# Three groups of weight sums made by DRAM-to-DRAM transfers, and three blocks of products recomposed

## The chip, the cores and the metric

The kernel runs on one core of a Trainium2 chip. A core has a matrix engine (TensorE, PE in the profile), a vector engine (VectorE, DVE), a scalar engine (ScalarE, ACT), a general engine (GpSimd, POOL) and SyncE (SP), which here only issues transfers. Each engine works through its own queue in order; semaphores make one wait for another. Sixteen DMA engines carry the transfers that SP, ACT and POOL issue. The metric is the device time of one execution in microseconds (us).

## The reference

One transformer block over 256 tokens of width 2048, in fp32. Three kinds of attention are mixed by gates, and a convolved, gated feed-forward layer follows:

```python
h = rms_norm(x, g_mix)
fq, fk, fv, f_logit, sq, sk, sv, mq, gates = split(h @ w_in)
o_fox = forgetting_attention(rms(fq), rms(fk), fv, cumsum(log_sigmoid(f_logit + b)))   # 6 heads of 128
o_sb = stick_breaking_attention(sq, sk, sv)                                            # 6 heads
mk, mv = split(rms_norm(mem, g_mem) @ w_mem_kv)
o_mem = memory_attention(rms(mq), rms(mk), mv)                                         # 4 heads
g = sigmoid(gates.reshape(..., 3, 2048) + b_gate)
x = x + (g[0] * (o_fox @ w_br_fox) + g[1] * (o_sb @ w_br_sb) + g[2] * (o_mem @ w_br_mem)) @ w_out
u = causal_depthwise_conv(rms_norm(x, g_ffn) @ w_up, conv_w, conv_b)                   # 2 x 5632 channels
x = x + (silu(u_gate) * u_val) @ w_down
```

Nearly all of the work is in the products with `w_in`, `w_out`, `w_up` and `w_down`.

## The kernel before

Each fp32 product is made of three matmuls in a faster format: both operands are split into a high and a low half, and `three` multiplies high by high, low by high and high by low (lines 360 to 362). A weight piece arrives by a DMA from SP ("raw"), ACT casts its high half ("hi", line 354, in the up stage line 143), DVE subtracts to get the low half ("lo", line 355 or 144), and PE then uses both. There are four buffers for hi and four for lo, and four to six for raw, so a piece can be some 5 us ahead of PE.

The stages follow one another: keys and values of the memory; the projections of the attentions; the gates (three blocks of 2048 columns, in two halves m = 0 and 1); the branches; the out stage; the up stage, in pieces of two k-tiles by 512 columns, eight for each group of four channel tiles; the down stage in two blocks of 1024 columns, "d0" and "d1".

In the gates, the out stage and the down stage, `blocked` works on pairs of k-tiles (128 rows each), two halves of the tokens and two halves of the columns. A pair is done in one of two ways. An **eight** (`eight`, "e" in a plan) multiplies the 2x2x2 blocks one by one: 8 products, 24 matmuls of 128x512, and splits two weight parts of 128x1024. A **seven** ("s") is a scheme of seven products with sums of activation blocks and sums of weight blocks: 21 matmuls. Its partial results gather in four more PSUM banks `Y`, and after the last seven of a block DVE spreads them (`gathered`, lines 1083 to 1095 for the gates; `gather` in the others).

- In the out and down stages, `seven` reads the weight sums T1 to T4 from DRAM tiles `kept_...`. They were made stages before, by SP loads into SBUF, three DVE adds and an SP store (`half_sums`, `pair_sums_ahead`, `first_sums`). A seven has parts of 1024, 1024, 1024 and 512 columns; the last, T4 (line 453), goes to a scratch tile.
- In the gates, `seven_here` uses sums that `prepared` makes on DVE one step ahead (lines 472 to 475, four adds of 128x512).
- The sums of activations come from `pair_sums` (five or more small DVE operations and ACT casts): for the gates ahead, in the background (`xs`, GS groups), in the down stage at the letter "f" of a plan. In d1 an "f" writes into places of the activations `aT` that d1's eights have used.

The scratch tiles have the name "junk" and rotate over two buffers:

```python
def junk(name):
    return sm.tile([P, 512], F32, tag="junk", bufs=2, name=name)
```

A tile that takes a buffer waits until the last user of that buffer is through. In the down stage, the T4 parts of all sevens are junk tiles.

What sets the order: a scheduler puts instructions on each engine's queue, and those passed to `in_order` keep the order of the program. `tick` runs one step of the generators in `background` and of the queued work (`later`). The up stage has 176 such ticks of 2.77 us.

## Time and profile before

| | us |
|---|---|
| median of 3 runs | 1461.15 (1460.55 to 1462.65) |
| profiled execution | 1460.56 |
| its span in the trace | 1458.8 |
| granted clock of TensorE | 1.000 |
| busy: PE / DVE / ACT / POOL | 1452.1 / 1221.8 / 851.9 / 21.4 |
| DMA | 387.64 MB, 266 GB/s on average |

Where the stages lie, from the trace: memory keys 0 to about 58; gate block 01 (half 0, branch 1) 361 to 402.7 and 02 to 444; up stage 742 to 1232; d0 to about 1344; d1 to 1453; then the last sums and the store.

The profile comes from one execution. In a row of the timeline stand the start, the duration, the engine, the line, the operation, output and inputs, and in brackets how long the engine was idle before and what ended that. A row of the windows gives for each engine the busy time in that stretch, then TensorE's granted clock, the share of the DMA engines' time, and GB/s. A row of PE's waits gives the sum, the number and the longest. The durations of matmuls overlap, and so do those of neighbouring DVE rows a little: the spacing of starts is what counts. A row of the DMA issues ends with the median time from issue to landing.

### The profile page before, as it was taken

Reading aid. Unit: us, or ns where it says so; the run is one execution under the profiler, and the core shown is the slowest. Engines: PE = TensorE matmul, PEld = TensorE weight load, DVE = VectorE, ACT = ScalarE, POOL = GpSimd, SP = SyncE. Lnnn points to the kernel's source line nnn. Section 1 sums busy time; section 2 is a strip of 40 time slices with the busy share of each in tenths; the row PEclk is TensorE's granted clock in tenths of the full one; section 3 lists DMA queues with packets and bytes.
Section 4 is the critical chain, followed back from the end, with each engine's and each line's share of the span. In section 5 each row is a group of like instructions: output and inputs, shape, how many; then the busy total and the mean of one; then the engine's idle time right before and its main releaser. Section 6 shows DMA issues by size and latency. Waiting matters only on the chain.

```text
span 1458.8 us, 20569 instructions
## 1 busy us (share of the span) xinstructions
PE 1452.1 (100%) x7295; PEld 1228.4 (84%) x7295; DVE 1221.8 (84%) x1804; ACT 851.9 (58%) x1210; POOL 21.4 (1%) x52
## 2 busy tenths in 40 slices
PE   9999999999999999999999999999999999999998
PEld 7888878888888888888888888888888888888887
DVE  5788778776898899998987888888888877999878
ACT  6755445464564555546766656556556565676665
POOL 0000010010000000000000000000000000000000
PEclk9999999999999999999999999999999999999999
DMA  8797899777668576788877888888888866789896
GB/s 290 228 352 247 320 323 333 266 250 217 212 206 268 176 226 201 271 266 261 304 213 231 290 275 299 282 270 299 286 278 298 272 197 201 253 283 341 293 334 220
DMA packets 166502, 387.64 MB, mean 266 GB/s; under 512 B 12554, under 2 KB 29854, under 8 KB 162174
## 3 DMA queue, kind: packets, MB, share of 16 engines
q1 hardware_dynamic: 164702, 383.29, 79.2%
q10 hardware_dynamic: 1328, 2.11, 0.4%
q8 instruction: 57, 0.93, 0.3%
q0 software_dynamic: 368, 0.93, 0.2%
q14 instruction: 47, 0.39, 0.1%
HBM read 347.47 MB, written 38.80 MB: 265 GB/s over the span
## 4 chain that ended last, share of the span: by engine, by line
PE 95%; issue 1%; DVE 1%; DMA 1%; SPq 0%; ACT 0%; POOL 0%; DVEq 0%; POOLq 0%; ACTq 0%
PE u L1289 22%; PE u L1290 11%; PE xg L362 4%; PE xg L361 4%; PE xg L360 4%; PE xd L360 4%; PE xd L362 3%; PE xd L361 3%; PE s L362 2%; PE f L360 2%; PE s L360 2%; PE f L362 2%; PE f L361 2%; PE b L362 2%; PE s L361 2%; PE b L361 2%
## 5 line engine op out<-in xcount | busy, mean ns | idle before, releaser
L1289 PE MATMUL u<-hT,hi_u 128*128 128x512 f32 x1232 | 428.5, 394 | 0.0
L1290 PE MATMUL u<-hT,lo_u 128*128 128x256 f32 x1232 | 341.5, 277 | 0.0
L1289 PEld LDWEIGHTS u<-hT,hi_u 128*128 128x128 f32 x1232 | 231.0, 188 | 53.4
L144 DVE TENSOR_TENSOR lo_u<-raw_u,hi_u 128x1024 fp32r<-128x1024 f32 x176 | 215.5, 1225 | 72.1 <-ACT hi_u L143 71.8
L143 ACT CAST hi_u<-raw_u 128x1024 fp32r<-128x1024 f32 x176 | 184.7, 1050 | 132.7 <-PE u L1289 107.0
L1290 PEld LDWEIGHTS u<-hT,lo_u 128*128 128x128 f32 x1232 | 231.5, 188 | 0.0
L355 DVE TENSOR_TENSOR lo_d<-raw_d,hi_d 128x1024 fp32r<-128x1024 f32 x88 | 106.8, 1223 | 16.7 <-ACT hi_d L354 14.3
L354 ACT CAST hi_d<-raw_d 128x1024 fp32r<-128x1024 f32 x88 | 91.8, 1053 | 39.9 <-PE xd L361 14.3
L354 ACT CAST hi_g<-raw_g 128x1024 fp32r<-128x1024 f32 (+1 forms) x80 | 77.0, 972 | 48.5 <-PE xg L361 19.2
L355 DVE TENSOR_TENSOR lo_g<-raw_g,hi_g 128x1024 fp32r<-128x1024 f32 (+1 forms) x80 | 88.7, 1121 | 4.1 <-ACT hi_g L354 4.1
L362 PE MATMUL xg<-lo_g,xT 128*128 128x512 f32 x175 | 68.1, 389 | 0.0
L360 PE MATMUL xg<-hi_g,xT 128*128 128x512 f32 x175 | 68.1, 389 | 0.0
L361 PE MATMUL xg<-hi_g,xT 128*128 128x512 f32 x175 | 68.1, 389 | 0.0
L143 ACT CAST hi_f<-raw_f 128x1024 fp32r<-128x1024 f32 (+1 forms) x40 | 38.5, 966 | 46.3 <-PE f L361 30.7
L144 DVE TENSOR_TENSOR lo_s<-raw_s,hi_s 128x1024 fp32r<-128x1024 f32 (+1 forms) x40 | 44.5, 1119 | 24.4 <-ACT hi_s L143 24.4
L1289 PE MATMUL u<-hT_rest,hi_u 128*128 128x512 f32 x176 | 62.0, 394 | 0.0
L143 ACT CAST hi_s<-raw_s 128x1024 fp32r<-128x1024 f32 (+1 forms) x40 | 38.4, 962 | 38.2 <-PE s L361 26.5
L143 ACT CAST hi_b<-raw_b 128x1024 fp32r<-128x1024 f32 x32 | 33.7, 1052 | 45.4 <-PE b L361 18.6
L1240 ACT ACTIVATE y<-u,taps 128x256 f32<-128x256 f32 x88 | 49.5, 595 | 17.0 <-DVE u L1235 16.8
L144 DVE TENSOR_TENSOR lo_f<-raw_f,hi_f 128x1024 fp32r<-128x1024 f32 (+1 forms) x40 | 44.4, 1117 | 16.9 <-ACT hi_f L143 16.9
L360 PE MATMUL xd<-hi_d,aT 128*128 128x512 f32 x148 | 57.6, 389 | 0.0
L362 PE MATMUL xd<-lo_d,aT 128*128 128x512 f32 x148 | 57.6, 389 | 0.0
(551 smaller groups left out, 3484.0 us busy)
## 6 DMA issues: line engine op xcount, KB each, us to landing
raw_u<-in_w_up_dram SPq DMA_DIRECT2D x176, 512.0 KB, 4.8
raw_g<-in_w_in_dram SPq DMA_DIRECT2D x96, 512.0 KB, 4.5
raw_d<-in_w_down_dram SPq DMA_DIRECT2D x63, 512.0 KB, 5.6
pre_d<-in_w_down_dram SPq DMA_DIRECT2D x17, 1024.0 KB, 7.2
kept_d<-pre_d SPq DMA_DIRECT2D x17, 1024.0 KB, 6.7
raw_f<-in_w_in_dram SPq DMA_DIRECT2D x32, 512.0 KB, 5.8
raw_s<-in_w_in_dram SPq DMA_DIRECT2D x32, 512.0 KB, 6.1
raw_t_d<-kept_d SPq DMA_DIRECT2D x25, 512.0 KB, 5.8
```

Source lines behind the costliest of these rows:

```text
L143: pin(nc.scalar.copy(hi[:, :m], raw[:, :m]))
L144: pin(nc.vector.tensor_tensor(lo[:, :m], raw[:, :m], hi[:, :m].bitcast(F32), ALU.subtract))
L354: nc.scalar.copy(hi[:, :n], src)
L355: nc.vector.tensor_tensor(lo[:, :n], src, hi[:, :n].bitcast(F32), ALU.subtract)
L360: fix(nc.tensor.matmul(o, lhsT=ah, rhs=w[0], start=first, stop=False))
L361: fix(nc.tensor.matmul(o, lhsT=al, rhs=w[0], start=False, stop=False))
L362: fix(nc.tensor.matmul(o, lhsT=ah, rhs=w[1], start=False, stop=last))
L1240: nc.scalar.activation(y, u[:, 2:], AF.Identity, scale=tap(2), bias=tap(3))
L1289: nc.tensor.matmul(ps[i], lhsT=hi[:, j, c], rhs=hT(k + j), start=first, stop=False)
L1290: nc.tensor.matmul(ps[i][:, :S], lhsT=lo[:, j, c], rhs=hT(k + j)[:, :S], start=False, stop=last)
```

## The change

Three groups of weight sums are made by POOL's transfers instead of not at all, and the plans use them. The plans give three pairs more to sevens: one in gate block 01 (the new letter "t": `seven` with kept sums, inside a gate block) and two in d1, whose order of letters changes too, with five "f" where three were. `GS` goes from 3 to 4, so that a fourth group of activation sums is made ahead for each half of the gates.

`sums_in_hbm` copies one column of its last argument into a junk tile on POOL (a mark, which makes what follows wait for that argument), then copies a pair's weights (1 MB) from DRAM into the kept tile, and forms the sums by four accumulating transfers of 256 KB within DRAM. It is called once in the memory keys' stage, and twice by `last_sums` late in the up stage, at ticks 148 and 160.

```diff
-GS = 3
+GS = 4
...
-    g_plans = (("", "esesesee", "esesesee"), ("esesesee", "esesesee", "esesesee"))
+    g_plans = (("", "esesest" + "e", "esesesee"), ("esesesee", "esesesee", "esesesee"))
     d_plans = (
         "efefefef" + "sef" * 4 + "ssefsfssfssee",
-        "efefef" + "sss" + "esss" * 3 + "ssee",
+        "efsss" * 3 + "efssfsssssee",
     )
+    in_hbm = (("d", 1, 14), ("d", 1, 15))
...
         for pr in pairs(name, plan.count("s"))
+        if (name, nb, pr) not in in_hbm
...
+    def sums_in_hbm(name, nb, pr, w, c0, behind):
+        mark = junk(f"mark_{name}_{pr}")[:, :1]
+        in_order(nc.gpsimd.tensor_copy(mark, behind))
+        kept = kept_for(name, nb, pr)
+        b = by_k(w)[:, 2 * pr : 2 * pr + 2, c0 : c0 + PIECE].rearrange("p k (n c) -> p k n c", n=2)
+        in_order(nc.gpsimd.dma_start(kept.rearrange("p (k n) c -> p k n c", k=2), b))
+        for dst, src in ((0, b[:, 0, 1]), (1, b[:, 1, 1]), (3, kept[:, 0]), (2, kept[:, 3])):
+            in_order(nc.gpsimd.dma_start(kept[:, dst], src, accum_op=ALU.add))
+
+    def last_sums(delay, period):
+        for _ in range(delay):
+            yield
+        for name, nb, pr in in_hbm:
+            sums_in_hbm(name, nb, pr, w_down, nb * PIECE, a_done[-1][:, :1].bitcast(F32))
+            for _ in range(period):
+                yield
...
-                by_seven(sp[s], s == 0, s == ns - 1)
+                (seven if c == "t" else by_seven)(sp[s], s == 0, s == ns - 1)
...
             row_rstd(rstd_m, ssm, "m")
+            sums_in_hbm("g", "01", 3, w_in, C_GATE + D, rstd_m[:, :1])
...
+    a_done = []
+    background.append(last_sums(148, 12))
...
-            split_to(a_pair(f // 2)[:, f % 2], g)
+            a_done.append(a_pair(f // 2)[:, f % 2])
+            split_to(a_done[-1], g)
...
-        return a_blocks[:, 2 * (p - N0 + N1) + f // 2, :, f % 2]
+        i = 3 * (p - N0) + f
+        return a_blocks[:, 2 * N1 + i // 2, :, i % 2]
```

The accumulations wait for one another where the second reads what the first wrote: the first waits for the 1 MB copy, the third for the first, the fourth for the third.

How this moves instructions, at three places. In the orders below, a row is a line of the code, an operation, output and inputs with their numbers, and the shape; lines of the changed kernel from 355 on are 19 higher in `parts` and 20 higher in the gates.

**DVE, end of gate block 01.** `lo_g01` are low halves of eights (k-tiles 12 to 15) or of parts of the seven of k-tiles 6 and 7 with `lo_t`, `lo_t4`; `yg01` the partial results that are gathered into `gw` and `g`; `g02` belongs to the next block. Before:

```order
L355 TENSOR_TENSOR lo_g01_12_3713<-raw_g01_12_3710,hi_g01_12_3712 128x1024
L1083 SCALAR_TENSOR_TENSOR g_0_1_0_3729<-yg01_0_3501,scales_111,bg_0_1_3497 128x512
L355 TENSOR_TENSOR lo_g01_13_3737<-raw_g01_13_3734,hi_g01_13_3736 128x1024
L1088 TENSOR_TENSOR gw_0_1_3728<-gw_0_1_3728,yg01_1_3502 128x512
L355 TENSOR_TENSOR lo_g01_14_3759<-raw_g01_14_3756,hi_g01_14_3758 128x1024
L1090 TENSOR_TENSOR gw_0_1_3728<-gw_0_1_3728,yg01_2_3503 128x512
L355 TENSOR_TENSOR lo_g01_15_3779<-raw_g01_15_3776,hi_g01_15_3778 128x1024
```

And in the changed kernel:

```order
L374 TENSOR_TENSOR lo_g01_6_3736<-raw_g01_6_3726,hi_g01_6_3735 128x1024
L374 TENSOR_TENSOR lo_g01_7_3746<-raw_g01_7_3729,hi_g01_7_3745 128x1024
L374 TENSOR_TENSOR lo_t_g01_3_3756<-raw_t_g01_3_3731,hi_t_g01_3_3755 128x1024
L374 TENSOR_TENSOR lo_t4_g01_3_3766<-raw_t4_g01_3_3733,hi_t4_g01_3_3765 128x512
L1103 SCALAR_TENSOR_TENSOR g_0_1_0_3791<-yg01_0_3517,scales_111,bg_0_1_3513 128x512
L374 TENSOR_TENSOR lo_g01_14_3775<-raw_g01_14_3772,hi_g01_14_3774 128x1024
L374 TENSOR_TENSOR lo_g01_15_3799<-raw_g01_15_3796,hi_g01_15_3798 128x1024
L1108 TENSOR_TENSOR gw_0_1_3790<-gw_0_1_3790,yg01_1_3518 128x512
L374 TENSOR_TENSOR lo_g02_6_3833<-raw_g02_6_3830,hi_g02_6_3832 128x1024
```

Where two low halves stood there are four, and the gathering starts behind them, with one eight of its block left instead of two.

**SP, the up stage.** `raw_u36_1_14` is the last weight piece of channel tiles 36 to 39, `raw_u40_0_0` the first of 40 to 43; `raw_t4_d0` are the T4 parts of the first two sevens of d0 (junk tiles). Before, those two stood near the start of the stage:

```order
L142 DMA raw_u0_1_2_7032<-in_w_up_dram 128x2x512
L142 DMA raw_u0_1_4_7060<-in_w_up_dram 128x2x512
L453 DMA raw_t4_d0_0_11976<-kept_d0_0_2252 128x512
L453 DMA raw_t4_d0_1_12067<-kept_d0_1_2414 128x512
L142 DMA raw_u0_1_6_7082<-in_w_up_dram 128x2x512
```

In the changed kernel they stand late in it:

```order
L142 DMA raw_u36_1_12_11281<-in_w_up_dram 128x2x512
L142 DMA raw_u36_1_14_11303<-in_w_up_dram 128x2x512
L472 DMA raw_t4_d0_0_12018<-kept_d0_0_2260 128x512
L472 DMA raw_t4_d0_1_12109<-kept_d0_1_2422 128x512
L142 DMA raw_u40_0_0_11337<-in_w_up_dram 128x2x512
L142 DMA raw_u40_0_2_11381<-in_w_up_dram 128x2x512
```

The two loads moved from the pieces of channel tile 0 to those of tile 40, since the marks take the two junk buffers first.

**POOL, the same place.** Before, nothing follows the two transfers at the start of the up stage. In the changed kernel (an "x2" stands for two transfers in a row):

```order
L1181 DMA rbc_5984<-rstd_row_6931 128x256
L326 COPY mark_d_14_11028<-aT_6779 128x1
L329 DMA kept_d1_14_11030<-in_w_down_dram 256x1x1024
L331 DMA kept_d1_14_11030<-in_w_down_dram 128x512 x2
L331 DMA kept_d1_14_11030<-kept_d1_14_11030 128x512 x2
L326 COPY mark_d_15_11325<-aT_6779 128x1
L329 DMA kept_d1_15_11327<-in_w_down_dram 256x1x1024
```

The second mark stands behind all five transfers of the first group.

More of the change, by code (lines that the diff above doesn't have):

```diff
@@ L403, in blocked @@
         Y = []
-        ns = plan.count("s")
+        ns = plan.count("s") + plan.count("t")
         def a_of(p, j, t):
@@ L451, in seven @@
             nc.sync.dma_start(raw2.rearrange("p (n c) -> p n c", n=2), kept[:, 0:4:3])
-            raw3 = t4_tile(f"raw_t4_{name}{nb}_{p}")
+            raw3 = t4_tile(f"raw_t4_{name}{nb}_{p}")[:, :512]
             nc.sync.dma_start(raw3, kept[:, T4])
@@ L496, in blocked @@
         s, e = 0, 0
-        sp = pairs(name, ns)
+        sp = range(ns) if name == "g" else pairs(name, ns)
         ep = [p for p in range(len(plan) - plan.count("f")) if p not in sp]
         for i, c in enumerate(plan):
-            if c == "s":
+            if c in "st":
                 if s == 0:
```

## The prediction

> **What bounds the kernel now.** I read the page's table of engines first, then PE's waits, then the timeline of PE, and only then the three places that the change touches. The engines' row of the page, and the whole list of what PE waited for:

> ```profile
> PE 1452.1 (100%) x7295; PEld 1228.4 (84%) x7295; DVE 1221.8 (84%) x1804; ACT 851.9 (58%) x1210; POOL 21.4 (1%) x52
> PE spare L93 <- DVE qscale L565: 1.2, 1, 1.2
> PE s L362 <- DVE lo_s L144: 0.8, 1, 0.8
> PE kv L155 <- DVE memT L186: 0.4, 1, 0.4
> PE kv L154 <- ACT memT L183: 0.3, 1, 0.3
> ```

> PE is busy for 1452.1 of 1458.8 us and waits 2.7 us in all, 1.9 of them at the start. So the time is the number of matmuls times their spacing: a removed matmul pays whatever the stage, and any new wait of PE is paid in full. The spacing is read where PE runs without a gap:

> ```profile
> 439.73 0.39 PE L361 MATMUL xg<-hi_g,xT_rest 128*128 128x512 f32 x1
> ...
> 444.26 0.39 PE L360 MATMUL b<-hi_b,oT 128*128 128x512 f32 x1
> ```

> Twenty matmuls start between 439.73 and 444.26: 0.2265 us each, although one is shown as 0.39 long, since they overlap.

> **Term 1, the removed matmuls: -2.04 us.** An eight has 24 products of 128x512, a seven 21. Three eights become sevens (one in the gates' block 01, two in the second down block), so nine matmuls go: 9 x 0.2265 = 2.04 us, 0.14% of the time. Nothing else in the change takes work from PE, so this is the whole gain. A measurement of this kernel tells about 0.2% (2.9 us) from no change; a gain by itself lies under that. The question is what PE has to wait for in exchange.

> **Term 2, the end of gate block 01: DVE.** The new seven has four parts to split where the eight had two, and DVE makes the low half of each. The next block's first seven follows soon behind it. DVE there, and PE's first two uses of that seven:

> ```profile
> 389.29 1.22 DVE L355 TENSOR_TENSOR lo_g<-raw_g,hi_g 128x1024 fp32r<-128x1024 f32 x1
> ...
> 398.75 0.69 DVE L472 TENSOR_TENSOR t_g<-raw_g 128x512 f32<-128x512 f32 x1 [0.58 <-DMA raw_g<-in_w_in_dram]
> ...
> 406.25 0.69 DVE L355 TENSOR_TENSOR lo_g<-raw_g,hi_g 128x512 fp32r<-128x512 f32 x1
> 406.86 0.69 DVE L475 TENSOR_TENSOR t_g<-t_g,raw_g 128x512 f32<-128x512 f32 x1
> 407.46 1.23 DVE L355 TENSOR_TENSOR lo_g<-raw_g,hi_g 128x1024 fp32r<-128x1024 f32 x1
> 408.59 2.36 DVE L355 TENSOR_TENSOR lo_t_g<-t_g,hi_t_g 128x1024 fp32r<-128x1024 f32 x2
> 408.58 0.39 PE L362 MATMUL yg<-lo_g,xT 128*128 128x512 f32 x1
> 409.26 0.39 PE L362 MATMUL xg<-lo_g,xT 128*128 128x512 f32 x1
> ```

> From 389.29 on, where the replaced eight's first split starts, DVE pauses once (0.58, for a DMA) before it is through with the second part at 407.46 + 1.23 = 408.69. PE wants that part at 409.26, so 0.57 us are spare. A split of 1024 occupies DVE for 1.13 (407.46 to 408.59), one of 512 for 0.61 (406.25 to 406.86). The new seven splits three of 1024 and one of 512, 3 x 1.13 + 0.61 = 4.00 us, against 2 x 1.13 = 2.26 for the eight: 1.74 more. The other DVE rows between those two points (the gathering of the block's sums, its scaling, the next block's weight sums) are the same ones in another order. PE for its part comes 3 x 0.2265 = 0.68 earlier. So DVE is late by 1.74 + 0.68 = 2.42, less the pause of 0.58 and the spare 0.57 if both are used up: 1.27 us. That is the lower bound. The upper one keeps the pause, and lets it grow by a little since the transfers stand in the same queue: 2.42 - 0.57 + 0.8 = 2.65. I take +2.0. The fourth set of activation sums that this block needs is made early, beside the gate projection:

> ```profile
> 345.00:365.00 20.00, 20.00 (x90) 16.55 (x89) 11.76 (x16) 8.98 (x10) 0.00 (x0) 1.00 0.58 172
> L369 DVE TENSOR_TENSOR xa<-xT x3: 686/691/692, 164.0 to 311.4; 128x512 f32<-128x512 f32 x3
> ```

> With this add of 0.69 us and four more operations that are no larger it costs DVE at most 5 x 0.69 = 3.5 us, where DVE is idle for 8 of 20: nothing on the path. The cover is that idle time; without it PE would wait up to those 3.5.

> **Term 3, the end of the up stage: SP's queue behind POOL.** Each of the two groups of weight sums begins with a POOL copy into a scratch tile of one column (the mark), which takes the next of two rotating scratch buffers. The first two sevens of the down stage load their last part into the same two buffers, so these two SP loads must now wait for the two marks. In the order of SP they stand between the last piece of channels 36 to 39 and the first of 40 to 43, and what is queued behind them is the whole weight stream of the stage. Before, they were issued at 754.78, long ahead, and the stream ran freely:

> ```profile
> 754.78 0.95 SPq L453 DMA_DIRECT2D raw_t_d<-kept_d  x2
> 1168.07 0.37 SPq L142 DMA_DIRECT2D raw_u<-in_w_up_dram  x1
> 1172.12 0.37 SPq L142 DMA_DIRECT2D raw_u<-in_w_up_dram  x1
> 1157.31 0.41 ACT L177 CAST aT<-y 128x256 fp32r<-128x256 f32 x1 [1.63 <-DVE y L1248]
> 1179.59 1.05 ACT L143 CAST hi_u<-raw_u 128x1024 fp32r<-128x1024 f32 x1 [1.72 <-PE u L1289]
> 1180.68 1.22 DVE L144 TENSOR_TENSOR lo_u<-raw_u,hi_u 128x1024 fp32r<-128x1024 f32 x1 [1.55 <-ACT hi_u L143]
> 1188.02 0.27 PE L1290 MATMUL u<-hT,lo_u 128*128 128x256 f32 x1
> ```

> The first mark waits for the cast that ends at 1157.72, so POOL starts at about 1158.0. The second mark stands on POOL's queue behind the first group's transfers: a copy of 1 MB from DRAM to DRAM, whose landing the first accumulating transfer (256 KB) waits for, whose landing the third waits for, whose landing the fourth waits for before it is issued. The second mark is then free after copy + 2 accumulations + about 1.0 us of issuing and the mark itself. No such transfer is in this trace. The nearest rows, first POOL's own, then SP's (KB each, us to landing):

> ```profile
> ck<-ck_row POOLq DMA_DIRECT2D x1, 512.0 KB, 9.4
> ck<-ck_row POOLq DMA_DIRECT2D x1, 256.0 KB, 7.6
> rbc<-rstd_row POOLq DMA_DIRECT2D x1, 128.0 KB, 6.4
> pre_d<-in_w_down_dram SPq DMA_DIRECT2D x17, 1024.0 KB, 7.2
> raw_d<-kept_d SPq DMA_DIRECT2D x25, 256.0 KB, 5.2
> raw_u<-in_w_up_dram SPq DMA_DIRECT2D x176, 512.0 KB, 4.8
> ```

> Cheapest, by SP's rows: 7.2 + 2 x 5.2 + 1.0 = 18.6, so the second mark comes at 1176.6. Dearest, POOL's line carried on (1.8 more for each 256 KB, so 13.0 for 1 MB) and 8 for an accumulation: 30.0, at 1188.0. I take POOL's rows at their nearest sizes, 9.4 + 2 x 7.6 + 1.0 = 25.6, at 1183.6. SP then issues the held load (0.5) and the first piece of channel 40, which lands 4.8 later; cast and split follow in 2.31 (1179.59 to 1181.90). PE wants it at 1188.02. So the stall is mark + 7.6 - 1188.0: nothing up to a mark at 1180.4, 3.2 us at 1183.6, 7.6 at 1188.0. I take +3.2. The 5 to 7 us that the piece had in hand are the cover here.

> [...]

> **Term 4, the second down block: +0.2 us.** Its last run of sevens grows from five to seven. What the run strains is the transfers:

> ```profile
> 1415.00:1440.00 25.00, 25.00 (x112) 20.69 (x111) 19.66 (x18) 17.20 (x20) 0.00 (x0) 1.00 1.00 349
> ACT hi_d L354 <- DMA raw_d<-in_w_down_dram: 0.6, 2, 0.4
> ```

> The DMA engines are busy throughout. A seven brings 1.835 MB in 21 x 0.2265 = 4.76 us, 385 GB/s, and gets 349. In the fifth seven ACT's cast already waits up to 0.4 us for a load. Two more sevens move that by 0.3 to 0.5 each, against some 1.5 us between a split and its use, of which the fifth seven's third part kept 0.9. Between 0 and 0.5; I take 0.2. The two more forms (activation sums, at most 3.5 us of DVE each, as above) and their copies on ACT, which wait for PE to be through with an eight, stand early in the block, where the next parts are cast ahead; nothing.

> **Term 5, the group made in the memory keys' stage: 0.** It adds a copy and four accumulations on POOL's queue at about 37 us, and on that queue nothing is wanted until 183. Its bytes share the engines with the stage's loads:

> ```profile
> 37.00:47.00 10.00, 10.00 (x53) 8.27 (x52) 7.44 (x10) 5.45 (x11) 0.00 (x0) 1.00 0.80 256
> 1150.00:1175.00 25.00, 25.00 (x147) 21.88 (x146) 22.89 (x38) 15.79 (x26) 0.00 (x0) 1.00 0.80 259
> ```

> A share of 0.80 leaves a fifth free, in both places. If the free fifth were not enough, loads there would come later by a few us at most, and I allow 0.3.

> **Sum.** -2.04 + 2.0 + 3.2 + 0.2 = +3.4 us. The profiled execution took 1460.56 (1458.8 and 1.8 around the span), so 1463.9 for one like it; the median of the three runs stands 0.6 above it, so 1464.5 as a median.

> **Rivals.**
> - Only the gates stall. POOL's transfers are as fast as SP's, the mark comes by 1180.4, SP's held loads are issued in time. Then -2.04 + 2.0 + 0.2 = +0.2: 1461.3. For it: SP's 1 MB in 7.2. Against it: every transfer of POOL in the trace takes longer than one of SP of its size. [...]
> - The covers all hold, and the change gives what it removes: 1461.15 - 2.0 = 1459.1. This is the other side. It turns on DVE at 389 to 409: it must win back 2.42 us, which it can only if PE's stall at the end of the new seven is absorbed by a wait that is shorter than I read, or the loads come earlier and the splits start before 389.29, together with a mark before 1180.4. Nothing in the rows speaks for the first.
> - The chain of transfers is long, at the dear end: -2.04 + 2.65 + 7.6 + 0.5 = +8.7, 1469.9. For it: an accumulation has to read what it adds to, which no row here prices.
> - The sums do not pay since the run of sevens becomes bound by transfers: two more sevens at 349 GB/s take 5.26 instead of 4.76 us each. With seven in a row that is 3.5 us behind, less 1.5 in hand: up to +2 in place of the 0.2. Against it: before's five in a row should then have cost 1 us, and PE has no wait there.

> **How the numbers follow.** Both stalls, gates and SP's queue: 0.55. Gates alone: 0.25. All covers hold: 0.14. Something else (the run of sevens, the memory keys' stage, another order of late things): 0.06. Of the first case, the part with a mark before 1183.1 stays under +2.9 us: 0.15 of the 0.55. Of the last, 0.04 are slower and 0.02 faster. So slower by over 0.2%: 0.40 + 0.04 = 0.44; faster: 0.02 and 0.01 taken from the covers that hold, 0.03, since it needs more than the removed matmuls; within 0.2%: 0.15 + 0.25 + 0.13 = 0.53. The range takes in all covers holding at the low end and the dear chain at the high end: 1459.0 to 1470.0. The most likely case by itself runs from 1461.5 to 1470.

> **What would show it.** PE's list of waits should gain two rows: a matmul of the gates' block 02 that waits for DVE's lo_g for 1 to 2.7 us at about 407 to 409, and one on L1290's successor that waits for lo_u by some 3 us at about 1188. SP's timeline should show a hole between the pieces around 1168, ended by a POOL copy. POOL's DMA rows should show 9 and 7 us. Wrong would be: no hole in SP, the accumulations in 3 us, no wait of PE at 408, or waits of PE behind 1415 for lo_d or lo_t_d.

## The result

The changed kernel takes 1469.76 us in the median of six runs (1467.88 to 1472.12), the kernel before 1460.96 us beside it (1460.13 to 1462.65): a ratio of 1.0061, 95% interval 1.0048 to 1.0074. It is 8.8 us slower. The forecast was 1464.5, slower by 3.4, in a range up to 1470: the direction and the place were right, the size was too small by more than half. By its chances the prediction even held no clear change for likelier (0.53) than a clear loss (0.44). That the time still lies inside the range, 0.2 us below its end, is luck: the end was set by a chain of transfers longer than the one that came.

The profiled execution of the changed kernel is the fastest of the six, 1467.88 us with a span of 1466.2, so its trace explains 7.4 of the 8.8 us; what the slower five had besides is not known. In three of the versions below one execution of eleven stands 7 to 9 us above the median at full clock.

### The profile page after: what moved, and what is told of

Read it like the earlier page. It is cut to its first block, busy times and chain, and to the rows that moved or that the text cites. A ratio compares the mean times of both kernels' runs of the same rounds, so it can differ in the third digit from the quotient of the medians.

```text
span 1466.2 us, 20656 instructions
## 1 busy us (share of the span) xinstructions
PE 1453.6 (99%) x7286; PEld 1230.5 (84%) x7286; DVE 1232.1 (84%) x1831; ACT 859.0 (59%) x1225; POOL 34.5 (2%) x70
## 4 chain that ended last, share of the span: by engine, by line
PE 91%; DMA 4%; DVE 2%; ACT 1%; issue 1%; SPq 0%; POOL 0%; ACTq 0%; DVEq 0%; POOLq 0%
PE u L1312 20%; PE u L1313 10%; PE xg L381 4%; PE xg L380 4%; PE xg L379 4%; PE xd L380 3%; PE xd L379 3%; PE xd L381 3%; PE f L379 2%; PE f L381 2%; PE f L380 2%; PE s L381 2%; PE s L379 2%; PE s L380 2%; PE b L380 2%; PE b L381 2%
## 5 line engine op out<-in xcount | busy, mean ns | idle before, releaser
L1313 PE MATMUL u<-hT,lo_u 128*128 128x256 f32 x1232 | 345.8, 281 | 0.5 <-DVE lo_u L144 0.5
L144 DVE TENSOR_TENSOR lo_u<-raw_u,hi_u 128x1024 fp32r<-128x1024 f32 x176 | 214.9, 1222 | 79.9 <-ACT hi_u L143 79.8
L143 ACT CAST hi_u<-raw_u 128x1024 fp32r<-128x1024 f32 x176 | 184.6, 1050 | 138.5 <-PE u L1312 89.0
L143 ACT CAST hi_f<-raw_f 128x1024 fp32r<-128x1024 f32 (+1 forms) x40 | 38.5, 967 | 47.7 <-PE f L380 26.2
L380 PE MATMUL xg<-hi_g,xT 128*128 128x512 f32 x168 | 65.4, 389 | 0.0
L379 PE MATMUL xg<-hi_g,xT 128*128 128x512 f32 x168 | 65.4, 389 | 0.0
L144 DVE TENSOR_TENSOR lo_s<-raw_s,hi_s 128x1024 fp32r<-128x1024 f32 (+1 forms) x40 | 44.4, 1120 | 23.1 <-ACT hi_s L143 23.1
L143 ACT CAST hi_s<-raw_s 128x1024 fp32r<-128x1024 f32 (+1 forms) x40 | 38.3, 962 | 42.6 <-PE s L380 26.7
L143 ACT CAST hi_b<-raw_b 128x1024 fp32r<-128x1024 f32 x32 | 33.7, 1052 | 44.2 <-PE b L380 20.2
L144 DVE TENSOR_TENSOR lo_f<-raw_f,hi_f 128x1024 fp32r<-128x1024 f32 (+1 forms) x40 | 44.4, 1117 | 17.7 <-ACT hi_f L143 14.9
L373 ACT CAST hi_t_d<-raw_t_d 128x1024 fp32r<-128x1024 f32 (+1 forms) x54 | 43.5, 836 | 19.3 <-PE xd L380 12.1
L373 ACT CAST hi_t_g<-t_g 128x1024 fp32r<-128x1024 f32 x30 | 31.6, 1052 | 38.8 <-PE xg L380 30.9
## 6 DMA issues: line engine op xcount, KB each, us to landing
raw_u<-in_w_up_dram SPq DMA_DIRECT2D x176, 512.0 KB, 4.9
raw_g<-in_w_in_dram SPq DMA_DIRECT2D x95, 512.0 KB, 4.4
raw_d<-in_w_down_dram SPq DMA_DIRECT2D x61, 512.0 KB, 5.9
pre_d<-in_w_down_dram SPq DMA_DIRECT2D x17, 1024.0 KB, 7.5
kept_d<-pre_d SPq DMA_DIRECT2D x17, 1024.0 KB, 6.0
raw_f<-in_w_in_dram SPq DMA_DIRECT2D x32, 512.0 KB, 5.7
raw_s<-in_w_in_dram SPq DMA_DIRECT2D x32, 512.0 KB, 6.0
raw_t_d<-kept_d SPq DMA_DIRECT2D x27, 512.0 KB, 6.1
```

What stands on the lines that cost most here:

```text
L143: pin(nc.scalar.copy(hi[:, :m], raw[:, :m]))
L144: pin(nc.vector.tensor_tensor(lo[:, :m], raw[:, :m], hi[:, :m].bitcast(F32), ALU.subtract))
L373: nc.scalar.copy(hi[:, :n], src)
L379: fix(nc.tensor.matmul(o, lhsT=ah, rhs=w[0], start=first, stop=False))
L380: fix(nc.tensor.matmul(o, lhsT=al, rhs=w[0], start=False, stop=False))
L1313: nc.tensor.matmul(ps[i][:, :S], lhsT=lo[:, j, c], rhs=hT(k + j)[:, :S], start=False, stop=last)
```

## The profile after

The first row is that of the engines, the rest the whole list of what PE waited for in the changed kernel:

```profile
PE 1453.6 (99%) x7286; PEld 1230.5 (84%) x7286; DVE 1232.1 (84%) x1831; ACT 859.0 (59%) x1225; POOL 34.5 (2%) x70
PE u L1312 <- ACT hi_u L143: 4.2, 1, 4.2
PE spare L93 <- DVE qscale L584: 1.2, 1, 1.2
PE xg L381 <- DVE lo_g L374: 0.8, 1, 0.8
PE g L379 <- DVE sb L1009: 0.6, 1, 0.6
PE mq L381 <- DVE lo_mq L144: 0.5, 1, 0.5
PE yg L381 <- DVE lo_g L374: 0.5, 1, 0.5
PE u L1313 <- DVE lo_u L144: 0.5, 1, 0.5
PE kv L776 <- DVE memT L769: 0.3, 1, 0.3
PE kv L155 <- DVE memT L186: 0.2, 1, 0.2
```

There are nine matmuls fewer (7295 before), and new waits: 4.2 and 0.5 us in the up stage, 0.8 and 0.5 at the gates' block 02, 0.6 in the gates' first projection (g) and 0.5 in the memory queries (mq). The 0.8 us for lo_s are absent in this execution.

The end of the up stage, on POOL's queue and then on SP's:

```profile
1159.42 0.61 POOL L326 COPY mark_d<-aT 128x1 f32<-128x1 f32 x1 [387.00 <-ACT aT L177]
1159.97 0.68 POOL L329 DMA_DIRECT2D kept_d<-in_w_down_dram  x1
1168.57 1.76 POOL L331 DMA_DIRECT2D kept_d<-in_w_down_dram  x2 [7.92 <-DMA kept_d<-in_w_down_dram]
1176.81 0.81 POOL L331 DMA_DIRECT2D kept_d<-kept_d  x1 [6.48 <-DMA kept_d<-in_w_down_dram]
1182.53 0.81 POOL L331 DMA_DIRECT2D kept_d<-kept_d  x1 [4.91 <-DMA kept_d<-kept_d]
1183.06 0.48 POOL L326 COPY mark_d<-aT 128x1 f32<-128x1 f32 x1
1170.06 13.84 SPq L472 DMA_DIRECT2D raw_t_d<-kept_d  x2
1184.00 1.88 SPq L142 DMA_DIRECT2D raw_u<-in_w_up_dram  x3
```

POOL waits for three landings on the way, and comes to the second mark at 1183.06. SP sits with the two loads of the down stage from 1170.06 on, and the next weight piece is issued at 1184.00. What that does to ACT and PE, and to TensorE's clock (in the windows: PE's busy time, then PEld, DVE, ACT, POOL, the granted clock, the DMA share, GB/s):

```profile
1192.59 1.04 ACT L143 CAST hi_u<-raw_u 128x1024 fp32r<-128x1024 f32 x1 [11.65 <-DMA raw_u<-in_w_up_dram]
1193.69 0.79 PE L1312 MATMUL u<-hT,hi_u 128*128 128x512 f32 x1 [4.16 <-ACT hi_u L143]
1186.00:1189.00 3.00, 3.00 (x19) 2.63 (x18) 0.00 (x0) 0.00 (x0) 0.00 (x0) 1.00 0.86 264
1189.00:1194.00 5.00, 0.84 (x5) 0.50 (x3) 0.33 (x1) 1.04 (x1) 1.67 (x2) 0.81 1.03 380
1194.00:1196.00 2.00, 1.53 (x5) 0.95 (x5) 1.41 (x2) 1.31 (x2) 0.00 (x0) 0.50 1.07 384
1196.00:1198.00 2.00, 2.00 (x8) 1.71 (x8) 1.90 (x3) 1.32 (x3) 0.00 (x0) 0.50 1.17 212
1198.00:1200.00 2.00, 2.00 (x10) 1.69 (x10) 1.81 (x6) 1.52 (x3) 0.66 (x1) 0.76 1.01 319
```

PE waits 4.16 us. Its clock is at half from 1192.12 to 1198.95 (the edges come from narrower windows), so PE works at half clock for the last 5.3 us of that. PE is shown as busy there, but does 8 matmuls in 2 us where it did 19 in 3 us.

To add up what the waits cost with the refill of the pipeline and the slow clock, I summed, over stretches of 50 us, by how much the starts of matmuls lie farther apart than is usual for their shape. Against the kernel before, the up stage's end costs 7.2 us, the gates' block 02 1.8, the wait at 338 0.9, the one at 67 0.9; the wait for lo_s (1.0) is not there, and the start is 0.5 shorter. With the 2.0 us of the removed matmuls: -2.0 + 7.2 + 1.8 + 0.9 + 0.9 - 1.0 - 0.5 = 7.3, against 7.4 measured. Each of these sums is good to some 0.2 us.

## The experiments

Theory A: the loss is the second mark. It takes a scratch buffer that a load of the down stage wants, that load stands in SP's queue ahead of the weight stream, and the mark stands on POOL's queue behind the first group's landings. Theory B: POOL's 4 MB take bandwidth from the weight stream. A third suspicion is that the gates' part carries the loss.

**Marks first.** Both marks ahead of the transfers; the scratch buffers are shared as before, and the transfers stay:

```diff
         for name, nb, pr in in_hbm:
-            sums_in_hbm(name, nb, pr, w_down, nb * PIECE, a_done[-1][:, :1].bitcast(F32))
+            mark_for(name, pr, a_done[-1][:, :1].bitcast(F32))
+        for name, nb, pr in in_hbm:
+            sums_in_hbm(name, nb, pr, w_down, nb * PIECE, None)
```

> The changed kernel, but both marks are made on POOL before the first group's transfers. The marks stay in the two scratch buffers that the first sevens' loads want, the transfers and their bytes stay. Theory A (SP's weight stream is held by a load that waits for the second mark, and the mark waits on POOL's queue for the first group's landings): the second mark comes at about 1160, SP has no hole, PE's waits of 4.2 and 0.5 us at 1189 to 1195 and the half clock after them (together 7.2 us in the trace of the changed kernel) are gone: about 1461, within 1 us of before. Theory B (the 4 MB that POOL moves there take bandwidth from the weight stream): the same transfers at the same time, so PE still waits about 4 us: 1467 to 1471.

Measured: 1461.21 us, ratio to before 1.0007 (0.9994 to 1.0020; before 1460.31 beside it). POOL, SP and PE's waits in this kernel:

```profile
1158.24 0.94 POOL L326 COPY mark_d<-aT 128x1 f32<-128x1 f32 x2 [386.80 <-ACT aT L177]
1183.74 1.02 POOL L333 DMA_DIRECT2D kept_d<-in_w_down_dram  x1
1158.88 0.81 SPq L478 DMA_DIRECT2D raw_t_d<-kept_d  x2
PE xg L387 <- DVE lo_g L380: 0.8, 1, 0.8
PE mq L387 <- DVE lo_mq L144: 0.5, 1, 0.5
PE yg L387 <- DVE lo_g L380: 0.5, 1, 0.5
PE mq L385 <- ACT hi_mq L143: 0.3, 1, 0.3
```

The two loads wait until 1158.9 and are gone; the second group's copy starts at 1183.74, as late as in the changed kernel, and PE does not wait in the up stage. Theory A holds and B falls: the same transfers at the same time cost PE nothing.

**A tile of its own for the marks.**

```diff
-        mark = junk(f"mark_{name}_{pr}")[:, :1]
+        mark = sm.tile([P, 1], F32, tag="mark", bufs=2, name=f"mark_{name}_{pr}")
```

> The changed kernel with the marks in a tile of their own, so that the two loads of the first sevens stand early in SP's order again, as before the change; POOL's queue is that of the changed kernel, with the second mark behind the first group. Theory A: no hole in SP's stream and no wait of PE at the end of the up stage, about 1461, as with the marks first. Theory B: as slow as the changed kernel, 1467 to 1471.

Measured: 1471.46 us, 1.0079 (1.0065 to 1.0093). Neither theory had this right: there is no wait of PE in the up stage (A), and the time is as long as B said. PE's longest new wait is 0.8 us, and it has a clock of 1.0. Instead, its matmuls are farther apart, 0.233 us in the down stage instead of 0.227. I put the new tile at 64 bytes of each partition, by which all tiles behind it in memory, the activations of the branches, the out stage and the down stage among them, begin later. No trace shows an address or that size (two buffers of one column alone hold 8 bytes): the shift is read from the tile and from the order in which the kernel opens its pools. That it costs time was a guess at this point; two runs test it.

**The marks in a tile that is there and unused** (160 columns that nothing reads):

```diff
-        mark = junk(f"mark_{name}_{pr}")[:, :1]
+        mark = sm_pad[:, pr : pr + 1]
```

> The changed kernel with the marks in a column of a tile that exists already and is used for nothing else, so that no other tile moves and the sevens' scratch buffers stay free. If the loss of the own mark tile (1471.5, with TensorE's spacing of 128x512 at 0.233 us instead of 0.227 in the stages whose activations that tile had shifted by 64 bytes) came from the shift alone, and theory A holds, this runs like the kernel with the marks first: 1460.5 to 1462, no wait of PE at the end of the up stage, spacing 0.227 in the down stage. If it came from the waiting marks or from POOL's transfers beside the early loads, it stays near 1470.

Measured: 1461.00 us, 1.0000 (0.9991 to 1.0009; before 1460.76). No wait of PE in the up stage, and the spacing in the down stage is 0.227. With the marks first the loads kept their late place in SP's order, and only the second mark came early; here the mark comes late (1181.95), and the loads need not wait for it. Both take the 7 us away. So the cause is that SP's queue held a load that waited for the second mark, and the own tile's loss came from where it lay.

**The kernel before, with that unused tile 64 bytes longer** and nothing else:

```diff
-    sm_pad = sm.tile([P, 160], F32, tag="pad", bufs=1, name="sm_pad")
+    sm_pad = sm.tile([P, 176], F32, tag="pad", bufs=1, name="sm_pad")
```

> The kernel before, with the unused tile 64 bytes longer, so that all tiles behind it lie 64 bytes further on, as the own mark tile had shifted them. No other instruction or size differs. If the shift alone makes the matmuls with these tiles slower (0.233 instead of 0.227 us each in the branches, the out stage and the down stage, some 1500 matmuls): 1468 to 1471. If the own mark tile's loss had another cause: 1460.8.

Measured: 1471.82 us, 1.0073 (1.0060 to 1.0086; before 1460.89). The engines' row, and two rows of PE's timeline between which 21 matmuls of 128x512 start:

```profile
PE 1463.7 (100%) x7295; PEld 1227.1 (83%) x7295; DVE 1223.8 (83%) x1804; ACT 851.2 (58%) x1210; POOL 21.4 (1%) x52
...
1400.03 0.39 PE L362 MATMUL xd<-lo_t_d,aT 128*128 128x512 f32 x1
...
1404.91 0.39 PE L362 MATMUL xd<-lo_t_d,aT 128*128 128x512 f32 x1
```

The same 7295 matmuls keep PE busy for 11.6 us longer: (1404.91 - 1400.03) / 21 = 0.232 us each, where the kernel before has 0.2265. The time is a little above the range that I expected.

**The down stage's part alone** (gates as before the change; marks as in the change):

```diff
-GS = 4
+GS = 3
-    g_plans = (("", "esesest" + "e", "esesesee"), ("esesesee", "esesesee", "esesesee"))
+    g_plans = (("", "esesesee", "esesesee"), ("esesesee", "esesesee", "esesesee"))
-            sums_in_hbm("g", "01", 3, w_in, C_GATE + D, rstd_m[:, :1])
```

> Only the down stage's part of the change (two groups at the up stage's end, the second down block's plan); gates as before. Two eights become sevens, -1.36 us. Theory A: plus 7.2 us for the hole, the refill and the half clock, up to 2 more where the mark is later: 1466.5 to 1470. If the gates' part carried most of the loss instead, this would stand below 1463.

Measured: 1467.98 us, 1.0050 (1.0038 to 1.0063), with the wait for hi_u at 3.8 us and the half clock behind it (6.8 us, as in the changed kernel). The down stage's part carries the loss.

**The gates' part alone** (down stage as before the change):

```diff
-        "efsss" * 3 + "efssfsssssee",
+        "efefef" + "sss" + "esss" * 3 + "ssee",
-    in_hbm = (("d", 1, 14), ("d", 1, 15))
+    in_hbm = ()
```

> Only the gates' part (one group in the memory keys' stage, the fourth set of activation sums, the new seven). -0.68 us for three matmuls, +1.8 for PE's waits at 408 to 411 (0.8 and 0.5 us of waiting, 1.76 with the refill), and 0 to 1 for small waits that appeared at 67 and 338: 1462 to 1463. If the gates' part cost nothing on a median, 1460.3.

Measured: 1462.34 us, 1.0017 (1.0004 to 1.0029): 2.0 us slower for three matmuls fewer. The third suspicion falls, but the part loses.

**The new seven earlier in its block**, with the marks in the unused tile:

```diff
-    g_plans = (("", "esesest" + "e", "esesesee"), ("esesesee", "esesesee", "esesesee"))
+    g_plans = (("", "estsesee", "esesesee"), ("esesesee", "esesesee", "esesesee"))
-            sums_in_hbm("g", "01", 3, w_in, C_GATE + D, rstd_m[:, :1])
+            sums_in_hbm("g", "01", 1, w_in, C_GATE + D, rstd_m[:, :1])
```

> The marks as in the kernel before this one, and the new seven of gate block 01 as its fourth letter instead of its seventh (e s t s e s e e), so that the block ends as it did before the change. If the waits at 408 to 411 (1.3 us, 1.76 with the refill) come from DVE being late at the block's end, they go, and no new ones appear where the seven stands now, since an eight follows it soon: 1.8 us less than with the marks alone, 1459 to 1460. If DVE's work of the whole block is too much for it, the waits only move to about 385 to 400: no gain.

Measured: 1459.45 us, 0.9993 (0.9984 to 1.0002), and once more, beside another set of runs of the kernel before:

> The kernel with the marks in the unused tile and the new seven as fourth letter once more, to narrow its interval beside the one with the down stage's part alone. If the gates' part now gains its three matmuls, 0.7 less than that one; if its waits at 67 and 338 eat them, the same.

1460.03 us, 0.9996 (0.9987 to 1.0004). The waits at 408 to 411 are gone in both traces, and no wait is listed in the gates' blocks in their place (by the starts of matmuls 0.2 to 0.4 us are lost around 390). Others appear, though: 0.4 and 0.5 us for lo_mq, and in the first of the two

```profile
PE g L379 <- DVE sb L1009: 1.4, 2, 0.8
```

in the gates' first projection. Against the kernel with only the marks moved the gain is 1.5 us in medians of the same set, which no interval separates from zero.

**The gates' group of weight sums at 112 us** instead of 37, added to the last:

```diff
-            sums_in_hbm("g", "01", 1, w_in, C_GATE + D, rstd_m[:, :1])
...
         if c == 0:
+            sums_in_hbm("g", "01", 1, w_in, C_GATE + D, y[:, 0, :1])
```

> As the kernel before this one, and the gates' group of weight sums is made at about 112 us instead of 37, where the DMA engines moved 247 GB/s. If the wait of PE for lo_mq at 67 us (0.5, with refill 0.9) comes from that group's transfers beside the loads, it goes and comes back nowhere: 0.5 to 1 less, 1458.3 to 1459.3. If it is chance, no change.

Measured: 1459.88 us, 0.9997 (0.9986 to 1.0008): no gain in time, where 0.5 to 1 us was expected. In the trace the wait for lo_mq is gone. The windows of the same stretch, of the changed kernel and then of this one:

```profile
46.00:56.00 10.00, 10.00 (x53) 8.17 (x52) 6.84 (x11) 6.68 (x11) 0.81 (x1) 1.00 1.05 282
```

```profile
46.00:56.00 10.00, 10.00 (x53) 8.18 (x52) 7.73 (x13) 6.97 (x12) 0.00 (x0) 1.00 0.58 162
```

The group takes the DMA share from 0.58 to 1.05 there. Of the eight traces with the group at 37 us seven have a wait for lo_mq (0.3 to 0.5 us), of the five without it there none. So the wait comes from the group, though not in every execution; that the time gains from moving it is not shown.

**Marks that wait for channel tile 34** instead of 35, in the changed kernel:

```diff
-            sums_in_hbm(name, nb, pr, w_down, nb * PIECE, a_done[-1][:, :1].bitcast(F32))
+            sums_in_hbm(name, nb, pr, w_down, nb * PIECE, a_done[min(len(a_done) - 1, 34)][:, :1].bitcast(F32))
```

> The changed kernel, but the marks wait for channel tile 34 instead of 35, whose cast ends 3.8 us earlier. Theory A: the second mark comes at about 1179.3, SP goes on 3.8 us earlier, PE waits some 0.5 to 1.5 us instead of 4.7. The half clock should not come after so short a wait (there was none after the waits of 0.8 us in the gates): 1462 to 1464.5. If the half clock came from the hole in SP's stream and not from PE's idling, it would stay, and the time be 1464 to 1466.

Measured: 1469.25 us, 1.0054 (1.0036 to 1.0072): a miss. In the profiled execution (1471.54; the four took 1466.90 to 1472.59) all matmuls of the up stage were a little farther apart than in the other traces, some 8 us over the stage, and why is not known; so only the place itself is compared. PE's waits there are 1.1 and 0.8 us instead of 4.2 and 0.5, and by the starts of matmuls the place costs about 4 us instead of 7.2, so the earlier mark did shorten the wait. But the half clock came all the same, for 3.4 us instead of 6.8:

```profile
PE u L1312 <- ACT hi_u L143: 1.1, 1, 1.1
PE u L1313 <- DVE lo_u L144: 0.8, 1, 0.8
1196.00:1199.00 3.00, 1.14 (x6) 0.51 (x5) 1.23 (x1) 2.01 (x2) 1.41 (x2) 1.00 1.04 394
1199.00:1200.00 1.00, 1.00 (x4) 0.88 (x5) 0.89 (x1) 0.78 (x2) 0.00 (x0) 0.56 1.15 322
1200.00:1202.00 2.00, 2.00 (x8) 1.65 (x7) 1.95 (x4) 1.84 (x4) 0.00 (x0) 0.50 1.17 201
```

My expectation that so short a wait leaves the clock alone was wrong. The other reason that I had named, the hole in SP's stream itself, is not ruled out by a run; the last section counts PE's work before each fall of the clock.

**The down stage's part alone, with the marks in the unused tile:**

> Only the down stage's part of the change, with the marks in the unused tile. By the theory so far this part then costs nothing and removes six matmuls: 1.36 us less than before, 1459.2 to 1459.8, no wait of PE at the end of the up stage. If POOL's 4 MB or the longer run of sevens cost something that the waits don't list, it stands at 1460.5 or above.

Measured: 1460.06 us, 0.9991 (0.9983 to 1.0000; before 1460.89). PE waits nowhere in the up and the down stage; a wait of 0.6 us between the out and the up stage, for the residual (xres_again), stands in this trace and not in that of the kernel before. The gain is 0.8 of the 1.36 us, and its interval just reaches 1. It stands level with the full change with the marks and the seven moved (1460.03 in the same set). So no gain of the gates' part is seen, but the intervals, about 1.3 us each way, are too wide for its 0.7. No version was shown to be faster than the kernel before.

## Why the prediction was right, and where it was not

- **Term 1, nine matmuls:** right, 7286 for 7295.
- **Term 2, DVE at the end of gate block 01:** right in mechanism and nearly in size. Waits of 0.8 and 0.5 us at the two matmuls that were named, 1.8 us in all for +2.0. Between the same two points DVE in the changed kernel has one pause left, 0.19 us, so the bound that uses up the pause (1.27) was the nearer one; the refill after each wait was not in the sum. The pause, the end of DVE's lateness, and the two waits:

```profile
394.80 2.50 DVE L374 TENSOR_TENSOR lo_g<-raw_g,hi_g 128x1024 fp32r<-128x1024 f32 x2 [0.19 <-ACT hi_g L373]
...
409.51 1.22 DVE L374 TENSOR_TENSOR lo_g<-raw_g,hi_g 128x1024 fp32r<-128x1024 f32 x1
409.05 0.50 PE L381 MATMUL yg<-lo_g,xT 128*128 128x512 f32 x1 [0.50 <-DVE lo_g L374]
410.79 0.50 PE L381 MATMUL xg<-lo_g,xT 128*128 128x512 f32 x1 [0.77 <-DVE lo_g L374]
```

  Moving the seven away from the block's end took the waits away.
- **The fourth set of activation sums, in term 2: "nothing on the path".** This step failed in part. I took the stretch from 345 to 365 as its place. In the changed kernel its five DVE rows stand between 322 and 336.4, the last right ahead of work of an attention (sb) that PE waits for:

```profile
335.68 0.69 DVE L397 TENSOR_TENSOR xs<-xr,xs 128x512 fp32r<-128x512 f32 x1
336.28 0.55 DVE L1009 TENSOR_TENSOR sb<-sb,r 128x384 f32<-128x384 f32 x1
```

  In that execution it cost 0.9 us; with the marks first, and with the marks in the unused tile, the same order cost nothing, and with the seven moved 1.4 us of waits in one trace and none in the other. That these rows are the cause was not tested by a run of its own.
- **Term 3, SP's queue behind POOL:** the chain was right, the price was not: 7.2 us for the 3.2. The second mark came at 1183.06 (forecast 1183.6), in part since two errors cancel: the first mark was 1.4 us later than forecast, and the chain took 23.6 us for 25.6, with 8.6 for the copy and 8.2 and 5.7 for the two accumulations, for 9.4 and twice 7.6. Two links of the sum were too small. The piece needed 8.6 us from issue to cast (1184.00 to 1192.59), for the 4.8 that I took from the median: SP issued one piece after the other once it was free, beside the second copy, and the windows show a DMA share of 1.03. And the sum ended when PE had its data again. The clock fell during the wait of 4.16 us and stayed at half for 6.8; with the clock at half PE lost some 1.9 of the 7.2 us (a 128x512 and a 128x256 matmul together took 0.64 us from start to start there, 0.35 at full clock). The sum had no term for that.
- **Term 4, the second down block: +0.2.** PE has no wait behind 1200, so 0. The windows show that the transfers got more than they had before, 363 GB/s at a share of 1.03 in the same 25 us, where the kernel before had 349:

```profile
1415.00:1440.00 25.00, 25.00 (x112) 20.68 (x111) 20.45 (x23) 18.30 (x22) 0.00 (x0) 1.00 1.03 363
```

- **Term 5, the group in the memory keys' stage: "0", at most 0.3.** Wrong: PE waited 0.5 us for lo_mq, 0.9 with the refill. The fifth of the DMA engines that the row for 37 to 47 showed free was not enough. The accumulations went on until about 62, and from 46 to 56 the group took the share from 0.58 to 1.05 (the two rows above), nearly half of the engines' time.
- **The rivals.** That POOL's transfers are as fast as SP's did not hold: 8.6 us for 1 MB and 5.7 to 8.2 for 256 KB, where SP's rows have 7.2 and 5.2. They ran beside the weight loads still under way, with the DMA engines' share at 0.71 to 1.06. The rival at 1469.9 gave nearly the right time for another reason: it had the mark at 1188.0, 4.9 us later than it came, and counted neither the late piece nor the clock.

## What to carry to other kernels

Before a small tile takes a buffer of a rotating pool, look who else takes from the pool and where that instruction stands in its engine's queue: here a copy of one column held the whole weight stream for 14 us. In a kernel that TensorE bounds, price a new wait with what comes after it (refill, a halved clock, late loads that then land together: here 7.2 us for waits of 4.2 and 0.5), not only until the data is there. And compare addresses before and after a change: 64 bytes cost 10.9 us here, and the change was to bring 2.0.

## What the runs showed of the hardware that I had not expected

- **64 bytes.** The kernel before took 1471.82 instead of 1460.89 us when the activations of three stages began 64 bytes later in each partition. The 128x512 matmuls of those stages started every 0.232 us instead of 0.2265; those of the gates, whose activations lie ahead of the longer tile, kept theirs (mean duration 389 ns in both traces, where the down stage's went from 389 to 394). In the down stage the sevens' products with activation sums, which lie in a tile that was not moved, were slower too, three of them in 0.693 us where three of the others took 0.700 and three before 0.680. So it is not settled that the address of a matmul's own operand decides.
- **The half clock.** It came with waits of 3.8 and 4.2 us, and in one execution with 1.1 and 0.8 us within 3 us. It did not come with 0.8 and 0.5 us within the same time in the gates. It lasts 6.83 us in the changed kernel and with the down stage's part alone, 3.41 with the marks for tile 34, and it begins 348, 347 and 350 times 3.413 us after the first record of the clock in the trace (at 4.28, 5.30 and 4.45 us). So the three traces fit steps of 3.41 us; why, no run shows. PE's work in three windows of that length, of the changed kernel and of the marks for tile 34, both right before the clock fell, and of the first version with the seven moved, where it did not fall:

```profile
1188.71:1192.12 3.41, 0.82 (x6) 0.46 (x4) 0.00 (x0) 0.00 (x0) 0.15 (x1) 1.00 1.02 393
1195.70:1199.11 3.41, 1.55 (x8) 0.87 (x7) 1.23 (x1) 2.09 (x2) 1.67 (x2) 1.00 1.05 395
337.94:341.35 3.41, 2.03 (x8) 1.12 (x7) 3.41 (x6) 1.71 (x3) 0.91 (x2) 1.00 0.87 191
```
